# Lending tiles to one attention head, and issuing three small steps later, in a two-layer trunk kernel

## The chip, the cores and the metric

The kernel runs on one core of a Trainium2 chip. The metric is the device time of one execution in microseconds (us), the median of several runs. The profiled execution comes with a trace of every instruction; its times count from the first instruction of the core.

## The reference

Two layers of the same block work on 512 frames of width 1024, in float32:

```
xn = rmsnorm(x);  [u | q | k | v | gA | gB] = xn @ w_in
q, k = rotary(rmsnorm(q)), rotary(rmsnorm(k))           # 4 heads, each of two q/k pairs of width 128
p_c  = softmax(q_c k_c^T / sqrt(128), chunk-causal)     # c = 0, 1
o    = rmsnorm((p_0 - lam * p_1) v)                     # v of width 256 a head
pool = (windowed mean of u, minus u) @ w_pool           # windows 2, 4, 8, 16: one for each 256 columns
x    = x + (sigmoid(gA) * pool + sigmoid(gB) * o) @ w_out
x    = x + SwiGLU(rmsnorm(x))
```

## The kernel before

Every float32 product is made of three TensorE matmuls (`product`: high x high, high x low, low x high), for which both operands are split into a rounded high part and a remainder. ScalarE (ACT) makes the high part, VectorE (DVE) the remainder (`split`, L216). Weights are loaded as float32 pieces (`raw`, seven slots) and split into `whi` and `wlo` (six slots).

The work goes head by head in the order 3, 2, 1, 0 (`ORDER`). `attention(j)` projects q and k of a head for the four blocks t of 128 tokens, then v and a gate. `merged(j-before)` then does the pooling branch of the head before: two products for u, two for its gate, and two small ones with `pw` (called y here). A layer ends with the feed-forward part.

The steps of a head that follow the q/k projection of a block t are these, with the lines of the profile:

- `evicted`: squares of the accumulator on ACT (L623), a mean and a power -0.5 on DVE and POOL (L355, L356). Then `normed`: the scaling into `qn` on ACT (L628), and in the same step the rotation on DVE (`rotate`, L385 and L393), a 32x32 transpose into the tile `near` (L326), a store to DRAM (`away<-near`, L327) and four loads back (L331), which together transpose the block.
- `turn`: the transposed `near` is scaled (L533) and split into `qh`, `ql`.
- `scores`: two products into the two `sc` banks, a maximum (L548), and Exp into a probability tile `pr` (L549). `joined` subtracts the second softmax from the first (L553 to L555) and sends the result through the same store and loads. Its transposed copy lies in the second half of the same `pr` tile.
- `turn_prob`: that copy is split into `ah`, `al`. `weighted`: the product with v (`mm<-vh,ah` and so on), squares (L588), scaling (L592). `turn_out` (L611) writes the head's rows of `mj`.

The first head of layer 0 (`at_start`) transposes on TensorE instead. In layer 1 the first head's projections of t = 0 and t = 1 are both held until the statistics of the tokens are there, so the steps of these two blocks start at the same moment.

The order of the work comes from the program and from a planner that runs when the program is built. `clock` counts the matmul columns issued. `later(delay, step)` puts a step into a heap, and `run_due` issues the steps whose time has come, between two products. `need(keys)` issues steps from the heap, in order of their time, until all the keys are ready, even before their time. So a step issued later takes a later place in each in-order engine queue. All delays are in columns. The tile framework then hands out slots, places instructions and inserts the waits: a tile of a tag with n slots waits until the tile that had the slot is no longer read.

Slots that matter here: `qn` three (used by `qn` and by its `near`), `pr` two, `ah` and `al` one each, `ta` two, `us` and `up` two each, `m` two, `mt` three (used by `mt` and its `near`), `sc` two banks, `mm` six banks.

The pooling branch (`windowed`) scales u into `up` (L689), adds shifted copies in `us` (L694, up to four times), finishes the mean (L697 to L700) and splits it into `uh`, `ul` at once. The gate is scaled into `ta` on DVE (L718) and goes through Tanh on ACT (L719) at once.

Of the kernel before, what the change touches and what calls it, by code (L numbers as in the profile page):

```python
# [11 lines left out]
F32R = mybir.dt.float32r  # L12
BF16 = mybir.dt.bfloat16
AF = mybir.ActivationFunctionType
# [4 lines left out]
P = 128  # L19
D = 1024  # L20
S = 512
# [32 lines left out]
SCORE_WAIT, PROB_WAIT, AV_WAIT, NORM_WAIT, MERGE_WAIT = 33600, 25200, 11400, 15000, 15000  # L54

QK_AWAY, SCORE_AWAY, PROB_AWAY, AV_AWAY, MERGE_AWAY = 28000, 26000, 32000, 18000, 24000
NORMED, JOINED, GATED = 4800, 2400, 4800
HIDDEN_DELAYS = (26000, 28000), (8000, 14000)


# [64 lines left out]
def trunk_kernel(  # L125
# [138 lines left out]
    def later(delay, what):  # L264
        heapq.heappush(waiting, (clock[0] + delay, count[0], what))
        count[0] += 1
# [97 lines left out]
    def need(*keys):  # L364
        run_due(lambda: all(k in ready for k in keys))
# [12 lines left out]
    def rotate(qn, t, layer):  # L378

        cs, sn = rotary[layer]  # L380
        both = sb.tile([P, 4, 4, ROT], F32, name="m12", tag="m12")

        def by(to, x, table):
            to, x = (v.rearrange("p (a h) r -> p a h r", a=2) for v in (to, x))
            nc.vector.tensor_mul(to, x, table.unsqueeze(2).broadcast_to(list(x.shape)))  # L385

        m1, m2 = both[:, 0], both[:, 1]
        by(m1, qn[:, :, :ROT], cs[:, :, t, :])
        for a in range(2):
            b = (1 - a) * HALF  # L390
            here = slice(a * HALF, (a + 1) * HALF)
            by(m2[:, :, here], qn[:, :, b:b + HALF], sn[:, :, t, here])
        nc.vector.tensor_add(qn[:, :, :ROT], m1, m2)  # L393
# [105 lines left out]
    for layer in range(L):  # L499
# [14 lines left out]
        def attention(j, before, then):  # L514

            if before is not None:
                need(*((layer, before, "s", t) for t in range(NT)))
            norm_eps = {}
            qh, ql = pair("q", "qk", 4)
            mj = sb.tile([P, 2, S], F32, name="mj", tag="mj", bufs=2)  # L520
# [16 lines left out]
            def scores(t):  # L537
                width = (t + 1) * P
                pr = sb.tile([P, 2, S], F32, name="pr", tag="pr", bufs=2)
                prob = [pr[:, c, :width] for c in range(2)]  # L540
                st = small("st", 2)
                mx = small("mx", 2)
                for c in range(2):
                    sc = s_ps()
                    product(sc[:, :width], [(
                        (qh[:, c, token(t)], ql[:, c, token(t)]), (qh[:, 2 + c, :width], ql[:, 2 + c, :width]))])
                    nc.vector.memset(sc[:CHUNK, width - CHUNK:width], MASKED)
                    nc.vector.tensor_reduce(mx[:, c:c + 1], sc[:, :width], axis=AX.X, op=ALU.max, negate=True)  # L548
                    nc.scalar.activation(prob[c], sc[:, :width], AF.Exp, bias=mx[:, c:c + 1], accum_out=st[:, c:c + 1])  # L549
                norm_eps[j, t] = rc = small("rc", 2)  # L550

                def joined():
                    nc.vector.reciprocal(rc[:, 1:2], st[:, 1:2])  # L553
                    nc.vector.scalar_tensor_tensor(rc[:, 0:1], rc[:, 1:2], st[:, 0:1], neglam[layer], op0=ALU.mult, op1=ALU.mult)
                    nc.vector.scalar_tensor_tensor(prob[0], prob[1], rc[:, 0:1], prob[0], op0=ALU.mult, op1=ALU.add)  # L555
                    nc.scalar.activation(rc[:, 1:2], st[:, 0:1], AF.Square, scale=EPS ** 0.5 / (1.0 - lam_init))
                    if at_start:
                        later(PROB_WAIT + (4000 if t == NT - 1 else 0) - JOINED, lambda: turn_prob(t, prob[0]))
                    else:
                        near = turned(prob[0], t + 1, near=prob[1])  # L560
                        later(PROB_AWAY - JOINED, lambda: turn_prob(t, near))
                    ready.add((layer, j, "s", t))

                after(JOINED, joined)

            def turn_prob(t, pr):
                if at_start:
                    tp = tr_ps()
                    for k in range(t + 1):
                        transpose(tp[:, token(k)], pr[:, token(k)])  # L570
                apart = at_start and t % 2
                ah, al = (sb.tile([P, S], F32R, name="a" + p, tag="u" if apart else "a" + p, bufs=2 if apart else 1) for p in "hl")
                width = (t + 1) * P
                if at_start:
                    split(ah[:, :width], al[:, :width], tp[:, :width])
                else:
                    split(*(squares_of(x[:, :width].rearrange("p (k c) -> p k c", c=P)) for x in (ah, al)), pr)
                later(AV_WAIT if at_start else AV_AWAY, lambda: weighted(t, ah, al))
# [32 lines left out]
                    nc.scalar.activation(into[:, a], src[:, a], AF.Copy, scale=gain_column(layer, 2 + a))  # L611
                ready.add((layer, j, "mj", t))

            at_start = not layer and j == ORDER[0]
            if not at_start:
                w = wblock(KD)
            held = []
# [1 line left out]
            def evicted(t, acc):  # L619
                qn = sb.tile([P, 4, QK], F32, name="qn", tag="qn", bufs=3)  # L620
                ss = small("ss4", 4)
                for h in range(4):
                    nc.scalar.activation(qn[:, h, :], acc[:, h * QK:(h + 1) * QK], AF.Square, accum_out=ss[:, h:h + 1])  # L623
                r = rsqrt_mean(ss, QK, 4, (QK ** -0.5, 1.0), [stats[0][:, i, t:t + 1] for i in (3, 4)])

                def normed():
                    for h in range(4):
                        nc.scalar.activation(qn[:, h, :], acc[:, h * QK:(h + 1) * QK], AF.Copy, scale=r[:, h:h + 1])  # L628
                    rotate(qn, t, layer)
                    near = qn if at_start else turned(qn.rearrange("p h c -> p (h c)"), 4, "qn", 3)  # L630
                    later((17400 + 5700 * t if at_start else QK_AWAY) - NORMED, lambda: turn(t, near))

                after(NORMED, normed)

# [49 lines left out]
        def windowed(j, c, acc, uh, ul):  # L684

            window = WINDOWS[j]
            up = sb.tile([P, 16 + S], F32, name="up", tag="up", bufs=2)
            nc.vector.memset(up[:, :16], 0.0)
            nc.vector.tensor_mul(up[:, 16:], acc, rms_rows[layer])  # L689
            prev, step, n = up, 1, 0  # L690
            while step < window:
                cur = sb.tile([P, 16 + S], F32, name="us", tag="us", bufs=2)
                nc.vector.memset(cur[:, :16], 0.0)
                nc.vector.tensor_add(cur[:, 16:], prev[:, 16:], prev[:, 16 - step:16 + S - step])  # L694
                prev, step, n = cur, step * 2, n + 1
            head = sb.tile([P, 16], F32, name="head", tag="head", bufs=2)
            nc.vector.tensor_mul(head, prev[:, 16:32], inv_t[:, j, :])  # L697
            nc.vector.scalar_tensor_tensor(
                prev[:, 32:], prev[:, 32:], 1.0 / window, up[:, 32:], op0=ALU.mult, op1=ALU.subtract)
            nc.vector.tensor_sub(prev[:, 16:32], head, up[:, 16:32])  # L700
            split(uh[:, c, :], ul[:, c, :], prev[:, 16:])

        def merged(j, mj, mh, ml):

            w = wblock(KD)
            pw = pool_weights(j)
            uh, ul = pair("u", "u", 2)
            for c in range(2):
                acc = mm_ps()
                product(acc, list(zip(cut(w, c * P, (c + 1) * P), x_all())))  # L710
                windowed(j, c, acc, uh, ul)

            gates = []
            for c in range(2):
                acc = mm_ps()
                product(acc, list(zip(cut(w, VD + c * P, VD + (c + 1) * P), x_all())))
                ta = sb.tile([P, S], F32, name="ta", tag="ta", bufs=2)
                nc.vector.tensor_mul(ta, acc, rms_rows[layer])  # L718
                nc.scalar.activation(ta, ta, AF.Tanh, scale=0.5)  # L719
                gates.append(ta)  # L720
            need(*((layer, j, "mj", t) for t in range(NT)))
            for c in range(2):
                y = mm_ps()
                product(y, list(zip(cut(pw, c * P, (c + 1) * P), [(uh[:, a, :], ul[:, a, :]) for a in range(2)])))
                ta = gates[c]
                k = KD * layer + 2 * j + c
                nc.vector.scalar_tensor_tensor(ta, ta, 1.0, y, op0=ALU.add, op1=ALU.mult)
                nc.vector.scalar_tensor_tensor(ta, ta, scale[:, k:k + 1], mj[:, c, :], op0=ALU.mult, op1=ALU.add)
                split_half(mh[:, c, :], ml[:, c, :], ta)
# [340 lines left out]
```

## Time and profile before

| what | value |
|---|---|
| runs | 1389.18, 1390.28 and 1390.07 us; median 1390.07 us |
| profiled execution | 1389.85 us |
| its span, first to last instruction | 1388.1 us, so 1.75 us lie around it |
| TensorE (PE) busy | 1375.9 us, 99%, 6242 matmuls |
| VectorE (DVE) busy | 999.4 us, 72% |
| ScalarE (ACT) busy | 777.8 us, 56% |
| GpSimd (POOL) busy | 123.8 us, 9% |
| mean granted TensorE clock | 0.997 of full speed |

Busy time of an engine is the time in which it has an instruction in work. The page's other parts name what ended each idle time (the releaser). A row of the timeline gives start, duration, engine, line, operation, output<-inputs, shape and count; square brackets at its end give the idle time before it and the releaser. SPq is the sequence of DMA issues of SyncE.

### The profile page before, as it was taken

What the parts mean: (1) busy time and instruction counts of PE and PEld (TensorE: products, weight loads), DVE (VectorE), ACT (ScalarE), POOL (GpSimd) and SP (SyncE); (2) the same over time, 40 slices, a digit from 0 to 9 for tenths busy, and PEclk for the clock granted to TensorE, in tenths of its full rate; (3) what the DMA queues carried; (4) which work ended last, traced back from release to release, by engine and by line L of the source; (5) the groups of instructions that cost most, each with busy time, mean ns of one, the idle gap of its engine ahead of it and who ended that gap; (6) DMA issues with size and microseconds to landing.
All of it is one profiled execution on the core that took longest, in us unless ns stands there. A gap on an engine that the chain in (4) does not pass through costs nothing.

```text
span 1388.1 us, 18670 instructions
## 1 busy us (share of the span) xinstructions
PE 1375.9 (99%) x6242; PEld 1140.2 (82%) x6242; DVE 999.4 (72%) x1787; ACT 777.8 (56%) x1577; POOL 123.8 (9%) x155
## 2 busy tenths in 40 slices
PE   9999999999999999999999989999999999999999
PEld 7888888888888888888888778888888888888887
DVE  7668677677869768678657676776878687686782
ACT  7665554554766555554456645555557565555540
POOL 3010100000101001110010001000001011001100
PEclk9999999999999999999999999999999999999999
DMA  8344454444668868676333545545436688687731
GB/s 310 99 130 134 126 159 130 148 135 136 148 181 193 240 174 232 157 207 202 119 129 120 147 128 153 152 121 149 154 115 152 184 199 230 184 219 175 199 127 61
DMA packets 141072, 224.07 MB, mean 161 GB/s; under 512 B 41392, under 2 KB 88496, under 8 KB 140976
## 3 DMA queue, kind: packets, MB, share of 16 engines
q1 hardware_dynamic: 130464, 187.20, 42.4%
q0 software_dynamic: 9216, 33.56, 14.1%
q10 hardware_dynamic: 1296, 2.13, 0.6%
q8 instruction: 49, 0.80, 0.2%
q14 instruction: 47, 0.39, 0.1%
HBM read 193.59 MB, written 29.23 MB: 161 GB/s over the span
## 4 chain that ended last, share of the span: by engine, by line
PE 96%; DVE 2%; issue 1%; ACT 1%; DMA 0%; SPq 0%; POOL 0%; DVEq 0%; ACTq 0%; POOLq 0%
PE mm L293 14%; PE mm L294 14%; PE mm L292 14%; PE mm L313 14%; PE mm L312 14%; PE mm L311 14%; PE sc L292 3%; PE sc L294 3%; PE sc L293 3%; PE sc L311 1%; PE sc L313 1%; PE sc L312 1%; DMA res<-in_x_t 0%; PE mm L318 0%; DVE wlo L216 0%
## 5 line engine op out<-in xcount | busy, mean ns | idle before, releaser
L216 DVE TENSOR_TENSOR wlo<-raw,whi 128x1024 fp32r<-128x1024 f32 (+1 forms) x221 | 267.4, 1215 | 79.4 <-ACT whi L216 78.7
L216 ACT CAST whi<-raw 128x1024 fp32r<-128x1024 f32 (+1 forms) x221 | 231.0, 1051 | 145.3 <-PE mm L294 61.2
L311 PE MATMUL mm<-whi,xh 128*128 128x512 f32 x480 | 189.0, 394 | 0.0
L313 PE MATMUL mm<-whi,xl 128*128 128x512 f32 x480 | 187.3, 390 | 0.0
L312 PE MATMUL mm<-wlo,xh 128*128 128x512 f32 x480 | 187.1, 390 | 0.0
L293 PE MATMUL mm<-fl,whi 128*128 128x512 f32 (+1 forms) x356 | 137.6, 387 | 0.0
L294 PE MATMUL mm<-fh,wlo 128*128 128x512 f32 (+1 forms) x356 | 137.6, 387 | 0.0
L292 PE MATMUL mm<-fh,whi 128*128 128x512 f32 (+1 forms) x356 | 137.6, 387 | 0.0
L732 DVE TENSOR_TENSOR res<-mm,res 128x512 f32<-128x512 f32 (+1 forms) x145 | 98.2, 680 | 46.4 <-PE mm L294 41.6
L313 PEld LDWEIGHTS mm<-whi,xl 128*128 128x128 f32 x480 | 90.1, 188 | 19.0
L312 PEld LDWEIGHTS mm<-wlo,xh 128*128 128x128 f32 x480 | 90.3, 188 | 17.4
L311 PEld LDWEIGHTS mm<-whi,xh 128*128 128x128 f32 x480 | 90.2, 188 | 17.3
L242 POOL DMA_DIRECT2D wlo<-in_wts x64 | 56.2, 878 | 536.5 <-ACT wlo L241 352.3
L312 PE MATMUL mm<-xl,whi 128*128 128x512 f32 x256 | 100.4, 392 | 0.0
L311 PE MATMUL mm<-xh,whi 128*128 128x512 f32 x256 | 100.3, 392 | 0.0
L313 PE MATMUL mm<-xh,wlo 128*128 128x512 f32 x256 | 100.1, 391 | 0.0
L356 POOL TENSOR_TENSOR r<-r,mhalf 128x4 f32<-128x4 f32 (+1 forms) x64 | 51.9, 814 | 531.1 <-DVE r L355 524.2
L292 PE MATMUL mm<-whi,xh 128*128 128x512 f32 x224 | 87.1, 389 | 0.0
L293 PE MATMUL mm<-wlo,xh 128*128 128x512 f32 x224 | 87.1, 389 | 0.0
L294 PE MATMUL mm<-whi,xl 128*128 128x512 f32 x224 | 87.1, 389 | 0.0
L241 ACT ACTIVATE wlo<-raw 128x1024 fp32r<-128x1024 f32 x64 | 67.9, 1060 | 29.2 <-PE mm L293 26.2
L292 PEld LDWEIGHTS mm<-fh,whi 128*128 128x128 f32 x356 | 66.9, 188 | 13.7
(221 smaller groups left out, 2969.1 us busy)
## 6 DMA issues: line engine op xcount, KB each, us to landing
raw<-in_wts SPq DMA_DIRECT2D x243, 512.0 KB, 4.0
wlo<-in_wts POOLq DMA_DIRECT2D x64, 512.0 KB, 6.3
away<-near SPq DMA_DIRECT2D x72, 256.0 KB, 2.3
near<-away SPq DMA_DIRECT2D x288, 64.0 KB, 2.9
away<-near SPq DMA_DIRECT2D x28, 128.0 KB, 1.9
near<-away SPq DMA_DIRECT2D x112, 32.0 KB, 2.0
pwr<-in_pool_w ACTq DMA_DIRECT2D x8, 256.0 KB, 3.2
away<-pr SPq DMA_DIRECT2D x7, 256.0 KB, 2.0
```

The source lines that it names most:

```text
L216: return nc.scalar.copy(hi, src), nc.vector.tensor_sub(lo, src, hi.bitcast(F32))
L241: made[0] = nc.scalar.activation(lo, raw, AF.Copy, scale=-1.0)
L242: nc.gpsimd.dma_start(lo.rearrange("p a b -> p (a b)"), wts[piece_no], accum_op=ALU.add)
L292: nc.tensor.matmul(acc, lhsT=ah, rhs=bh, start=start, stop=False, **check)
L293: nc.tensor.matmul(acc, lhsT=ah, rhs=bl, start=False, stop=False, **check)
L294: last = nc.tensor.matmul(acc, lhsT=al, rhs=bh, start=False, stop=stop, **check)
L311: nc.tensor.matmul(acc, lhsT=ah, rhs=bh, start=i == 0, stop=False)
L312: nc.tensor.matmul(acc, lhsT=ah, rhs=bl, start=False, stop=False)
L313: last = nc.tensor.matmul(acc, lhsT=al, rhs=bh, start=False, stop=i == n - 1)
L356: nc.gpsimd.tensor_tensor(r, r, mhalf[:, :width], op=ALU.pow)
L732: return nc.vector.tensor_add(res[d][:, cs], acc, res[d][:, cs])
```

## The change

Four things are done. In layer 1's head 3 (`roomy`), the transposed probabilities go to a `ta` tile instead of the second half of `pr`; `ah` and `al` of t = 1 and t = 3 share an `m` tile; and the `near` of q and k of t = 1 and t = 3 is a `us` tile instead of a `qn` one. In all heads, the scaling of q and k is issued 7200 columns after the squares, not 4800 (`NORMED`), and the rotation with its transpose and DMAs becomes a step of its own, another 2400 columns later (`ROTATED`); `turn` keeps its place. In all pooling branches the split of the pool sums is issued 9600 columns later (`SUMMED`) and the Tanh of the gate 2400 columns later (`GATE`). The y products are issued after `need` has found the two splits and the two Tanhs issued, as well as `mj`.

```diff
-NORMED, JOINED, GATED = 4800, 2400, 4800
+NORMED, ROTATED, JOINED, GATED, SUMMED, GATE = 7200, 2400, 2400, 4800, 9600, 2400
...
+            at_start = not layer and j == ORDER[0]
+            roomy = layer and j == ORDER[0]
...
-                        near = turned(prob[0], t + 1, near=prob[1])
+                        near = turned(prob[0], t + 1, *(("ta", 2) if roomy else ()), near=None if roomy else prob[1])
...
-                apart = at_start and t % 2
-                ah, al = (sb.tile([P, S], F32R, name="a" + p, tag="u" if apart else "a" + p, bufs=2 if apart else 1) for p in "hl")
+                if at_start and t % 2:
+                    ah, al = (sb.tile([P, S], F32R, name="a" + p, tag="u", bufs=2) for p in "hl")
+                elif roomy and t % 2:
+                    both = sb.tile([P, 2, S], F32R, name="a", tag="m", bufs=2)
+                    ah, al = both[:, 0, :], both[:, 1, :]
+                else:
+                    ah, al = (sb.tile([P, S], F32R, name="a" + p, tag="a" + p) for p in "hl")
...
                 def normed():
                     for h in range(4):
                         nc.scalar.activation(qn[:, h, :], acc[:, h * QK:(h + 1) * QK], AF.Copy, scale=r[:, h:h + 1])
+                    after(ROTATED, rotated)
+
+                def rotated():
                     rotate(qn, t, layer)
-                    near = qn if at_start else turned(qn.rearrange("p h c -> p (h c)"), 4, "qn", 3)
-                    later((17400 + 5700 * t if at_start else QK_AWAY) - NORMED, lambda: turn(t, near))
+                    tag = ("us", 2) if roomy and t % 2 else ("qn", 3)
+                    near = qn if at_start else turned(qn.rearrange("p h c -> p (h c)"), 4, *tag)
+                    later((17400 + 5700 * t if at_start else QK_AWAY) - NORMED - ROTATED, lambda: turn(t, near))
...
-            split(uh[:, c, :], ul[:, c, :], prev[:, 16:])
+
+            def rounded():
+                split(uh[:, c, :], ul[:, c, :], prev[:, 16:])
+                ready.add((layer, j, "u", c))
+
+            after(SUMMED, rounded)
...
-                nc.scalar.activation(ta, ta, AF.Tanh, scale=0.5)
                 gates.append(ta)
-            need(*((layer, j, "mj", t) for t in range(NT)))
+
+                def bent(c=c, ta=ta):
+                    nc.scalar.activation(ta, ta, AF.Tanh, scale=0.5)
+                    ready.add((layer, j, "g", c))
+
+                after(GATE, bent)
+            need(*((layer, j, "mj", t) for t in range(NT)), *((layer, j, x, c) for x in "ug" for c in range(2)))
```

More of the change, by code (lines that the diff above doesn't have):

```diff
@@ L612, in turn_out @@
                 ready.add((layer, j, "mj", t))
-            at_start = not layer and j == ORDER[0]
             if not at_start:
```

## The prediction

> **What bounds the kernel.** I read the page's first part, then PE's waits, the busy time by stretches, the timeline of PE where it waits, and from there backwards the timelines of the engines it waits for.
>
> ```profile
> span 1388.1 us, 18670 instructions
> PE 1375.9 (99%) x6242; PEld 1140.2 (82%) x6242; DVE 999.4 (72%) x1787; ACT 777.8 (56%) x1577; POOL 123.8 (9%) x155
> ```
>
> PE is busy for all but 12.2 us, so a change that removes no matmul can gain only there. The waits of PE by line and releaser (total, times, longest), and two stretches of busy time (count in brackets, then granted clock, DMA share, GB/s):
>
> ```profile
> PE mm L313 <- DVE al L216: 4.3, 2, 3.9
> PE mm L311 <- ACT ah L216: 2.5, 1, 2.5
> 85.00:140.00 55.00, 55.00 (x265) 46.37 (x264) 45.62 (x104) 33.71 (x84) 3.02 (x4) 1.00 0.51 153
> 804.10:810.90 6.80, 5.88 (x14) 4.61 (x15) 6.14 (x23) 2.50 (x9) 0.78 (x1) 0.50 0.17 37
> ```
>
> 6.8 us of waits are for `ah` and `al`, the split probabilities. The stretch of layer 0 in which head 2 and the pooling of head 3 run (85 to 140) has no idle PE. The stretch 804.1 to 810.9 in layer 1 ran at half the clock. PE's timeline at the places:
>
> ```profile
> 765.46 0.39 PE L313 MATMUL mm<-whi,xl 128*128 128x512 f32 x1
> 768.34 0.39 PE L311 MATMUL mm<-vh,ah 128*128 128x256 f32 x1 [2.49 <-ACT ah L216]
> 769.85 0.39 PE L313 MATMUL mm<-whi,xl 128*128 128x512 f32 x1
> 770.60 0.39 PE L313 MATMUL mm<-vh,al 128*128 128x256 f32 x1 [0.36 <-DVE al L216]
> 800.71 0.39 PE L311 MATMUL mm<-xh,whi 128*128 128x512 f32 x1
> 805.02 0.58 PE L313 MATMUL mm<-vh,al 128*128 128x256 f32 x1 [3.92 <-DVE al L216]
> 810.98 0.39 PE L313 MATMUL mm<-xh,wlo 128*128 128x512 f32 x1
> 811.21 0.40 PE L311 MATMUL mm<-xh,whi 128*128 128x512 f32 x1
> ```
>
> At full clock a 512-column matmul starts every 0.23 us (810.98 to 811.21). The three places cost, start to start less 0.23: 2.65, 0.52 and 4.08 us, together 7.25. From 805.02 to 810.98 there are 5.96 us for the stretch's 14 matmuls, one of 256 columns: at full pace 13.5 x 0.23 = 3.1, so the half clock cost 2.9. **Everything to be won is 10.1 us, in layer 1's head 3 and the head behind it.**
>
> **Why it waits.** The first stall, head 3, t = 3 (DVE and ACT rows):
>
> ```profile
> 746.31 0.69 DVE L548 TENSOR_REDUCE mx<-sc 128x1 f32<-128x512 f32 x1
> 753.98 0.43 DVE L216 TENSOR_TENSOR al<-pr,ah 128x256 fp32r<-128x256 f32 x1
> 755.57 0.68 ACT L549 ACTIVATE pr<-sc,mx 128x512 f32<-128x512 f32 x1
> 758.84 0.70 DVE L326 STREAM_TRANSPOSE pr<-pr 128x512 f32<-128x512 f32 x1
> 767.65 0.64 ACT L216 CAST ah<-pr 128x512 fp32r<-128x512 f32 x1
> 719.69 0.68 DVE L216 TENSOR_TENSOR ql<-near,qh 128x512 fp32r<-128x512 f32 x1
> 720.41 0.71 DVE L326 STREAM_TRANSPOSE near<-qn 128x512 f32<-128x512 f32 x1
> ```
>
> The maximum was there at 747.0, but the Exp of t = 3 began at 755.57: both `pr` slots were taken, and that of t = 1 came free with its `al` at 754.41. So 8.6 us passed before it, and 12.1 from Exp to `ah`. Likewise the transposed q and k of t = 2 (720.41) started right after the `ql` of t = 0 had freed a `qn` slot (720.37). The second stall, head 2, t = 0, and the same two steps in layer 0 as the last two rows:
>
> ```profile
> 779.71 0.31 DVE L326 STREAM_TRANSPOSE pr<-pr 128x128 f32<-128x128 f32 x1
> 785.10 1.73 SPq L327 DMA_DIRECT2D away<-near  x3
> 786.92 0.40 SPq L327 DMA_DIRECT2D away<-pr  x1
> 793.10 1.86 SPq L331 DMA_DIRECT2D pr<-away  x4
> 800.68 0.69 DVE L689 TENSOR_TENSOR up<-mm,hg 128x512 f32<-128x512 f32 x1 [2.20 <-PE mm L313]
> 804.68 0.28 DVE L216 TENSOR_TENSOR al<-pr,ah 128x128 fp32r<-128x128 f32 x1
> 105.00 0.28 DVE L216 TENSOR_TENSOR al<-pr,ah 128x128 fp32r<-128x128 f32 x1
> 113.84 0.28 PE L311 MATMUL mm<-vh,ah 128*128 128x256 f32 x1
> ```
>
> The store was issued 6.9 us after its data was transposed, since SP issues in order and had three other stores ahead (785.10); the loads came another 6.2 us later. `al` then stood in DVE's queue behind the pool sums, which stood 2.2 us for PE. In layer 0 the same `al` was done 8.5 us before its product.
>
> **The change, part by part.** No instruction, byte or DMA is added or removed; slots and places in queues change. 512 columns are 0.23 us, so 2400 are 1.1, 4800 are 2.1 and 9600 are 4.3.
>
> *Lent tiles.* With `near` in `ta`, `pr` of t = 1 is free once it is transposed, not once it is split, so the Exp of t = 3 can follow its maximum at 747.0: 8.6 us earlier. The split of t = 1 no longer waits for the product of t = 0 to read `ah`, which the `m` tile unties. The Exp-to-`ah` time of 12.1 us then ends near 759, and PE wants the data at 765.7: room of 6 us against a stall of 2.65. The lenders are idle by what they do: `ta` is next written by the gates of the pooling, `m` by its result, `us` by its sums, and these start no sooner than the row at 800.68. Gain: 2.65 + 0.52 = 3.2.
>
> The second stall: the late stores ahead of `away<-pr` are those of head 3 and of q and k of head 2, which queued behind them. If head 3 runs 8 us earlier, layer 1's head 2 should stand as layer 0's, with 8.5 us in hand. Gain: 4.08 + 2.9 = 7.0. What would be late next is the `mt` ring, which is not widened (rivals).
>
> *Rotation later (32 blocks).* Three waits that it addresses, and the rows of one block, from the first square to the scaled q:
>
> ```profile
> L385 DVE TENSOR_TENSOR m<-qn,hg 128x128 f32<-128x128 f32 x32 | 9.3, 290 | 28.1 <-ACT qn L628 27.7
> 62.34 0.28 ACT L623 ACTIVATE qn<-mm 128x128 f32<-128x128 f32 x1 [0.76 <-PE mm L313]
> 66.51 0.27 DVE L385 TENSOR_TENSOR m<-qn,hg 128x128 f32<-128x128 f32 x1
> 75.92 0.51 ACT L533 ACTIVATE near<-near,scale 128x256 f32<-128x256 f32 x1 [0.49 <-DMA near<-away]
> ```
>
> DVE stood 28.1 us at 32 rotations, 0.9 each, for ACT. A rotation already started 4.2 us after the squares (62.34 to 66.51); the new place is 9600 columns = 4.3 us after them. So it moves by 0.1 us if DVE arrives in time, and by 2.1 if all of the delay counts. `turn` stands where it stood, and the trip from rotation to `turn` took 9.4 us (66.51 to 75.92) with ACT waiting 0.5. A later rotation moves the transpose, one store and four loads on SP's queue with it; behind `turn` on ACT's queue stand weight roundings. Cost between 0 and what the rival below says; I take 0, being nearer to the row.
>
> *Pool sums and Tanh later.* 16 of each. The last row pair is `ul` and its first reader in layer 1's first pooling:
>
> ```profile
> L216 ACT CAST uh<-us 128x512 fp32r<-128x512 f32 x16 | 10.0, 623 | 44.5 <-DVE us L700 31.5 <-DVE us L693 13.0
> 822.09 0.69 DVE L216 TENSOR_TENSOR ul<-us,uh 128x512 fp32r<-128x512 f32 x1
> 827.94 0.39 PE L312 MATMUL mm<-ul,pw 128*128 128x512 f32 x1
> ```
>
> ACT stood 44.5 us at 16 roundings, 2.8 each; placed 4.3 later, it finds them ready. Even if `ul` were 4.3 us later than its end at 822.78, it would beat its reader by 0.9. The slot of `us` is held longer, but 4.3 us is less than the 5.5 (24 matmuls) until the next sums. The Tanh is 1.1 later and read only behind the y product, so its cover is that product; if it is gone, at most 1.1 us for the last pooling of each layer. `need` may now issue steps up to 1.1 us ahead of their time; against 8.5 us of margin, nothing. Lower bound for this part: PE has no wait for these, so no gain by itself, except that `al` no longer stands behind them.
>
> **Sum.** 1389.85 - 3.2 - 7.0 = 1379.7 for the profiled execution; I add 0.3 for one short wait at a weight split (the 0.7 us margin of the last rival). The median is 0.22 above that execution: **1380.2 us**.
>
> One rule to weigh: the half clock came after an idle time of 3.92 us and not after one of 2.49. [...]
>
> **Rivals.**
>
> *The second stall stays, whole.* `al` may still be queued behind the pool sums, which the change does not reorder by itself. Only 3.2 us are gained: 1390.1 - 3.2 = 1386.9. For it speaks that DVE is an in-order queue in the rows above; against it, layer 0.
>
> *The second stall stays, but short.* By the rows the half clock comes between 2.49 and 3.92 us of idle time. A rest of 1 to 3 us keeps the clock: 1381 to 1383.5.
>
> *Nothing moves.* The `mt` ring takes over: `near` of the attention output holds a slot until `turn_out`, and late `mt` tiles delay the same DVE and SP queues. The stalls return at other rows: within 1387.3 to 1392.8.
>
> *Slower.* Rotation and its trip late by all of the 2.1 us: `turn`, first in ACT's in-order queue, then waits 0.5 + 2.0 for its loads, and the roundings of weights behind it come late. The tightest one in the trace, at layer 1's head 3 (two splits, and the matmul that reads the second):
>
> ```profile
> 716.27 2.36 DVE L216 TENSOR_TENSOR wlo<-raw,whi 128x1024 fp32r<-128x1024 f32 x2
> 719.33 0.39 PE L312 MATMUL mm<-wlo,xh 128*128 128x512 f32 x1
> ```
>
> The margin is 0.7 us (718.63 to 719.33). A standstill of 1.3 us there costs 0.6. Eight heads have three such changes of weights each; were all as tight, 24 x 0.6 = 14.4 us, and 1390.1 - 10.1 + 14.4 = 1394.4. It decides from 0.54 us at every change (24 x 0.54 = 12.9 = the gain and 2.8 more). Against it: rotations were already 4.2 us behind the squares. [...]
>
> **How the numbers follow.** Differences of 0.2%, 2.8 us, are about what a measurement here can tell from none: 1387.3 to 1392.8 is no change. Forecast (both stalls gone) 0.63; second stall short 0.08; whole 0.09; nothing moves 0.10; slower 0.10. That gives faster 0.79 (the whole-stall case ends close to the bound), same 0.11, slower 0.10. The range takes in the first three cases, 0.80: up to 1387.2, which is the whole-stall case with the 0.3 added. Down to 1378.0: all 10.1 without the 0.3, the 0.9 by which the fastest run (1389.18) lies under the median, and 1.1 for shorter waits of the same stage that PE's busy time hides. The likeliest case alone: 1378.5 to 1381.5.
>
> **What would show it.** Right: PE without waits for `ah` and `al`, clock 1.00 from 737 to 832, the Exp of head 3's t = 3 within 2 us of its maximum, `away<-pr` of head 2's t = 0 within 2 us of its transpose, L385's and `uh`'s waits for ACT and DVE gone, and a span near 1378. Wrong: PE waiting for `wlo`, `ql` or `ul`; a stretch at half clock; L533 waiting for its loads far longer.

## The result and the profile after

In one job on one chip the kernel before took 1389.62 us (median of four executions, the three known before and one more) and the changed kernel 1380.59 us (1380.28 to 1381.05): ratio 0.9937, 95% interval 0.9920 to 0.9954. The forecast was 1380.2. The profiled execution of the changed kernel took 1380.28 us, against 1389.85 before. Page of the changed kernel, span and first part:

```profile
span 1378.5 us, 18671 instructions
PE 1371.7 (100%) x6242; PEld 1138.8 (83%) x6242; DVE 995.6 (72%) x1787; ACT 774.9 (56%) x1577; POOL 129.2 (9%) x155
```

These are the same matmuls in a span 9.6 us shorter. PE's waits in the changed kernel (line and releaser, total us, times, longest):

```profile
PE sc L311 <- ACT pr L551: 1.6, 2, 1.0
PE mm L408 <- DVE us L703: 1.2, 1, 1.2
PE mm L440 <- DVE sq L436: 0.4, 1, 0.4
PE mm L311 <- ACT ah L216: 0.2, 1, 0.2
```

6.8 us of waits for `ah` and `al` have become 0.2. A wait for a score bank is new: 1.6 us. Busy time by stretches, before (first fence) and after (second):

```profile
737.00:800.00 63.00, 60.15 (x283) 49.52 (x282) 43.11 (x102) 42.03 (x128) 6.39 (x8) 1.00 0.50 154
800.00:832.00 32.00, 28.00 (x123) 22.77 (x122) 25.61 (x62) 12.52 (x29) 2.30 (x3) 0.89 0.38 115
```

```profile
737.00:800.00 63.00, 61.99 (x294) 51.70 (x293) 44.51 (x107) 42.66 (x132) 6.94 (x9) 1.00 0.47 139
800.00:832.00 32.00, 31.83 (x153) 26.52 (x152) 26.55 (x64) 14.70 (x39) 3.01 (x4) 1.00 0.55 173
```

11 and 30 more matmuls fit into the two stretches, and the granted clock of the second is 1.00, not 0.89. The two chains, in the changed kernel. First head 3, t = 3, on DVE, ACT and PE:

```profile
742.10 1.29 DVE L550 TENSOR_REDUCE mx<-sc 128x1 f32<-128x512 f32 x2
742.83 0.69 ACT L551 ACTIVATE pr<-sc,mx 128x512 f32<-128x512 f32 x1
756.47 0.65 ACT L216 CAST a<-near 128x512 fp32r<-128x512 f32 x1
762.95 0.28 PE L311 MATMUL mm<-vh,a 128*128 128x256 f32 x1
```

The Exp follows its maximum at once; before it waited 8.6 us. The split starts at 756.47, not 767.65, and PE does not wait for it. Then head 2, t = 0: transpose, store, the store of t = 1, loads, split, and the matmul that reads `al`:

```profile
780.85 0.32 DVE L326 STREAM_TRANSPOSE pr<-pr 128x128 f32<-128x128 f32 x1
782.41 0.36 SPq L327 DMA_DIRECT2D away<-pr  x1
785.43 0.32 SPq L327 DMA_DIRECT2D away<-pr  x1
788.19 4.04 SPq L331 DMA_DIRECT2D pr<-away  x8
795.52 0.30 ACT L216 CAST ah<-pr 128x128 fp32r<-128x128 f32 x1
796.26 0.28 DVE L216 TENSOR_TENSOR al<-pr,ah 128x128 fp32r<-128x128 f32 x1
796.66 0.33 PE L313 MATMUL mm<-vh,al 128*128 128x256 f32 x1
```

There is no stall, but hardly any room: `al` ends at 796.54 and is read at 796.66.

The starts of the n-th matmul in both traces show where the time was gained. The changed kernel is 0.7 us ahead before the first stall and 4.1 ahead after it. It loses 1.5 near 779, is 2.7 ahead before the second stall, and 9.6 after it and at the end.

### The profile page after: what moved, and what is told of

Same layout as the page of the kernel before. It is cut to its first block, busy times and chain, and to the rows that moved or that the text cites. A ratio compares the mean times of both kernels' runs of the same rounds, so it can differ in the third digit from the quotient of the medians.

```text
span 1378.5 us, 18671 instructions
## 1 busy us (share of the span) xinstructions
PE 1371.7 (100%) x6242; PEld 1138.8 (83%) x6242; DVE 995.6 (72%) x1787; ACT 774.9 (56%) x1577; POOL 129.2 (9%) x155
## 4 chain that ended last, share of the span: by engine, by line
PE 95%; ACT 1%; DVE 1%; issue 1%; DMA 0%; POOL 0%; SPq 0%; ACTq 0%; DVEq 0%; POOLq 0%
PE mm L293 15%; PE mm L294 14%; PE mm L292 14%; PE mm L311 14%; PE mm L313 14%; PE mm L312 14%; PE sc L292 3%; PE sc L294 3%; PE sc L293 3%; PE sc L311 1%; PE sc L312 1%; ACT whi L216 1%; PE sc L313 1%; DVE wlo L216 0%; PE mm L318 0%
## 5 line engine op out<-in xcount | busy, mean ns | idle before, releaser
L356 POOL TENSOR_TENSOR r<-r,mhalf 128x4 f32<-128x4 f32 (+1 forms) x64 | 57.4, 898 | 516.7 <-DVE r L355 503.0
```

The source lines that it names most:

```text
L356: nc.gpsimd.tensor_tensor(r, r, mhalf[:, :width], op=ALU.pow)
```

## The experiments

Each ratio is to the kernel before in the same job. The code cuts show only the lines that differ, in e8 from the kernel of e1, in all others from the changed kernel.

**The parts apart.** Theory A: the slots of layer 1's head 3 caused everything. B: the second stall hangs on the place of the pool sums. C: the parts only work together.

```diff
 # e1_tiles_only
+NORMED, ROTATED, JOINED, GATED, SUMMED, GATE = 4800, 0, 2400, 4800, 0, 0
 # e2_delays_only
+            roomy = False
 # e3_no_sum_delay
+NORMED, ROTATED, JOINED, GATED, SUMMED, GATE = 7200, 2400, 2400, 4800, 0, 2400
 # e4_no_rot_delay
+NORMED, ROTATED, JOINED, GATED, SUMMED, GATE = 4800, 0, 2400, 4800, 9600, 2400
```

> Only the lent tiles; scaling, rotation, pool sums and Tanh in their old places. Theory A (the slots of layer 1's head 3 caused both stalls): both stalls and the half clock go, 1380 to 1382 us, waits of PE for ah and al under 1 us. Theory B (the second stall hangs on the place of the pool sums ahead of al in DVE's queue, and the lent tiles only cure the first): 3.2 us gained, about 1386.5, and the wait for al near 795 to 805 us of the span is still 3 to 4 us, with a stretch at half clock. Theory C (the parts only work together): 1388 to 1391.

Measured: 1380.47 us, 0.9933 (0.9916 to 0.9949). The lent tiles alone give all of the gain. PE's wait for `al` in that kernel:

```profile
PE mm L313 <- DVE al L216: 1.1, 2, 0.9
```

> All four later places, no lent tile. Theory A: the ring of pr, ah and al in layer 1's head 3 is as before, both stalls stay, 1387 to 1391. Theory B: the first stall stays (2.5 to 3.2 us), the second and its half clock go: about 1383. Theory C: 1388 to 1391, as A.

Measured: 1387.68 us, 0.9987 (0.9978 to 0.9997), at the edge of A and not B's 1383. All stalls are still there, some shorter, and one for an `ah` at 817.38 is new:

```profile
PE mm L311 <- ACT ah L216: 3.1, 2, 2.1
PE mm L313 <- DVE al L216: 1.8, 2, 1.5
800.00:832.00 32.00, 29.41 (x140) 23.41 (x139) 28.04 (x67) 14.35 (x34) 2.70 (x4) 1.00 0.46 146
```

In place of the wait of 3.9 us for `al` there is one of 1.5, with the new one of 1.0, and in this execution no half clock followed. That is where the 2 us come from.

> The changed kernel with the pool sums split at once again. Theory A: within 1.5 us of the changed kernel, 1380 to 1382. Theory B: a wait for al of 3 to 4 us near 800 us of the span returns, with the half clock 1387, without it 1384.

Measured: 1381.46 us, 0.9941 (0.9926 to 0.9956), as A.

> The changed kernel with scaling and rotation at their old places (4800 columns, in one step). Theory A: within 1.5 us of the changed kernel, 1380 to 1382; DVE's wait at the rotation returns to some 28 us in total, off PE's path. Theory C (the parts only work together): 1383 or more, with a PE wait for ah, al or a score in layer 1's first two heads.

Measured: 1380.61 us, 0.9934 (0.9919 to 0.9949), as A. PE's waits are those of the lent tiles alone (1.1 us for `al`), not the 1.6 us for a score bank. B and C have fallen.

**One loan less.**

```diff
 # e5_no_ta
+                        near = turned(prob[0], t + 1, near=prob[1])
 # e6_no_m
+                elif False:
 # e7_no_us
+                    tag = ("qn", 3)
```

> The changed kernel without the ta loan: the transposed probabilities of layer 1's head 3 lie in pr again. Theory A1 (each link of the chain pr, near, ah holds t = 3 by itself, and the ta loan is the one that frees pr): the Exp of t = 3 waits for the al of t = 1 again, and starts 4 to 9 us after its maximum; the first stall returns in part, 1382 to 1387. Theory A2 (any one of the loans makes enough room): 1380 to 1381.5.

Measured: 1391.40 us, 1.0011 (1.0002 to 1.0021): worse than either theory said, a little above the kernel before. PE at t = 3 of head 3, and the two stretches at half clock (0.50 and 0.51, the number after POOL's count):

```profile
765.56 0.39 PE L311 MATMUL mm<-vh,a 128*128 128x256 f32 x1 [1.77 <-ACT a L216]
766.85 0.58 PE L313 MATMUL mm<-vh,a 128*128 128x256 f32 x1 [0.78 <-DVE a L216]
766.40:769.80 3.40, 2.95 (x12) 2.86 (x13) 3.37 (x8) 2.29 (x4) 0.00 (x0) 0.50 0.09 10
807.30:810.70 3.40, 3.40 (x10) 2.62 (x9) 2.84 (x11) 1.20 (x6) 0.00 (x0) 0.51 0.02 5
```

The step that A1 named is not where most of it is lost. The way of t = 3, from its Exp to its split:

```profile
747.86 0.69 ACT L551 ACTIVATE pr<-sc,mx 128x512 f32<-128x512 f32 x1
754.71 0.34 SPq L327 DMA_DIRECT2D away<-near  x1
755.57 1.88 SPq L331 DMA_DIRECT2D pr<-away  x4
761.16 0.28 ACT L629 ACTIVATE qn<-mm 128x128 f32<-128x128 f32 x1 [3.14 <-PE mm L313]
764.88 0.63 ACT L216 CAST a<-pr 128x512 fp32r<-128x512 f32 x1
```

The Exp starts 1.3 us after its maximum (746.57), not 4 to 9, as the split of t = 1 is early with the `m` loan. But its loads stand behind a store of q and k (754.71) on SP, and its split on ACT behind squares that wait 3.14 us for PE. So the split comes at 764.88, 8.4 us later than in the changed kernel. The rows show this order; no run isolates it.

> The changed kernel without the m loan: ah and al of t = 1 and t = 3 share the one slot with t = 0 and t = 2 again. Theory A1: the split of t = 1 waits for the product of t = 0 near 752 us of the span, the ta slot of t = 1 comes free only then, and t = 3 is late again: 1382 to 1387. Theory A2: 1380 to 1381.5.

Measured: 1383.85 us, 0.9957 (0.9942 to 0.9972), as A1. The first stall is back, 2.17 us long. The Exp of t = 3 is on time (743.88), but the split of t = 1 waits (753.42), and with it the transpose of t = 3 for its `ta` tile (754.33).

> The changed kernel without the us loan: near of q and k of t = 1 and t = 3 takes a qn slot again. Theory A1: q of t = 2 and t = 3 is 4 us later as before, but a score is wanted only 8 us or more after that; no stall, 1380 to 1381.5. Theory A3 (the loan of us is what frees SP's queue and the second head): the wait for al near 800 us returns, 1383 or more.

Measured: 1387.52 us (1385.43 to 1389.28), 0.9984 (0.9975 to 0.9994). My A1 expectation was wrong by 6 us. The SP and ACT queues show why; first the changed kernel's SP, then that of the kernel without `us` (count at the end of each row), then its ACT:

```profile
745.24 3.00 SPq L327 DMA_DIRECT2D away<-near  x2
748.45 3.69 SPq L331 DMA_DIRECT2D near<-away  x8
```

```profile
747.60 1.83 SPq L331 DMA_DIRECT2D near<-away  x4
749.52 4.82 SPq L327 DMA_DIRECT2D away<-near  x2
754.45 0.37 SPq L228 DMA_DIRECT2D raw<-in_wts  x1
754.86 4.04 SPq L331 DMA_DIRECT2D near<-away  x8
760.62 0.28 ACT L629 ACTIVATE qn<-mm 128x128 f32<-128x128 f32 x1 [3.65 <-DVE near L326]
761.63 0.63 ACT L216 CAST a<-near 128x512 fp32r<-128x512 f32 x1
```

With the loan, the probabilities of t = 2 and t = 3 come back in one run of eight loads from 748.45. Without it, the loads of t = 3 stand behind a second store, which the row 749.52 stretches to 754.34, and come from 754.86. Then the split stands on ACT behind squares that wait 3.65 us for a `qn` slot: it starts at 761.63, not 756.47. PE still gets it in time; its new waits, for a score's `qh` (1.9 us) and an `ah` (2.2 us), are in head 2. How the lateness reaches head 2 is read from these rows, not isolated.

> The ta and m loans alone, no us loan, all steps in their old places. Theory I (without the us loan q and k of t = 2 and t = 3 are 5 us late, and this alone upsets the order of SP's and ACT's queues): about 1387, as without us in the changed kernel, PE waits for qh or ah of 4 to 6 us. Theory J (the us loan is needed only together with the later rotation, which lengthens the time in which a qn slot is held): 1380 to 1382.

This drops `us` from the lent tiles alone (the edits of e1 and e7). Measured: 1385.77 us, 0.9974 (0.9963 to 0.9984). The loan is worth about 5 us without any later step (1380.47 with it, in another job), so J has fallen; but the waits are for `al` (2.0 us) and `ah` (1.8), not `qh`.

**What is late next.** One more loan, `up` for the transposed attention output.

```diff
 # e8_mt_loan (on e1), e9_after_mt_loan (on the changed kernel)
-                        near = turned(m, 2, "mt", 3)
+                        near = turned(m, 2, *(("up", 2) if roomy else ("mt", 3)))
```

> The lent tiles alone, with one more loan: in layer 1's head 3 the transposed attention output lies in an up tile instead of an mt one. Theory D (the mt ring is what is late next: it holds the queues of DVE and SP, and so causes the rest of PE's waits for al, 1.1 us, in head 2): the transposes of the attention output of t = 2 and t = 3 come 8 to 12 us earlier, PE's waits for al fall under 0.4 us, 1379 to 1380. Theory E (these waits are from DVE's load by pool sums alone): as with the lent tiles alone, 1380 to 1381.

Measured: 1378.97 us (1378.74 to 1379.22), 0.9922 (0.9907 to 0.9937): D by its time, and the fastest of all. PE has no idle time left in either stretch. Its busy time there, then the squares of t = 3 and the transpose of t = 2 with the lent tiles alone, and with the further loan:

```profile
737.00:800.00 63.00, 63.00 (x300) 52.62 (x300) 45.77 (x119) 43.17 (x135) 6.98 (x9) 1.00 0.45 135
800.00:832.00 32.00, 32.00 (x154) 26.90 (x153) 27.17 (x65) 15.15 (x40) 3.48 (x4) 1.00 0.52 166
```

```profile
773.31 0.38 ACT L595 ACTIVATE mt<-mm 128x256 f32<-128x256 f32 x1
777.67 0.44 DVE L326 STREAM_TRANSPOSE near<-mt 128x256 f32<-128x256 f32 x1
```

```profile
765.26 0.39 ACT L595 ACTIVATE mt<-mm 128x256 f32<-128x256 f32 x1
773.24 0.45 DVE L326 STREAM_TRANSPOSE near<-mt 128x256 f32<-128x256 f32 x1 [0.35 <-ACT mj L618]
```

The squares come 8.0 us earlier, the transpose only 4.4, less than I wrote: with two `up` slots it still waits for `mj` of t = 0. That of t = 3 comes only 0.8 earlier (778.63 to 777.80). So D holds for the waits, not for the size of its steps.

> The changed kernel, delays and all, with the loan of an up tile for the transposed attention output as well. Theory D (the mt ring is what was late next in the changed kernel): the wait for a score near 778 us (1.6 us with its neighbours) goes, 1379 to 1379.8. Theory H (this wait comes from the later rotation, which puts q of the second block of head 2 late whatever the ring): it stays, 1380 to 1381, and the delays cost about 1 us beside the tiles with the mt loan (1378.97).

Measured: 1379.78 us, 0.9930 (0.9913 to 0.9946). The wait near 778 us is gone, as D says. It is also gone without the later scaling and rotation (e4), so it takes both, and H is right in that part. One for a score bank in layer 0, 0.6 us, is left, which no kernel with the rotation at its old place has; the changed kernel has it too, in this row:

```profile
54.65 0.38 PE L311 MATMUL sc<-qh 128*128 128x256 f32 x1 [0.60 <-ACT pr L551]
```

**The later steps by themselves.**

```diff
 # e11_sums_late_only
+NORMED, ROTATED, JOINED, GATED, SUMMED, GATE = 4800, 0, 2400, 4800, 9600, 0     (roomy = False)
 # e12_rot_later
+NORMED, ROTATED, JOINED, GATED, SUMMED, GATE = 7200, 7200, 2400, 4800, 9600, 2400
```

> The kernel before with one thing changed: the pool sums split 9600 columns later. Theory F (this is what the delays alone gained, 2 us, since al then waits less behind the pool sums in DVE's queue and the half clock does not come): 1387 to 1388.5, no half clock. Theory G (the gain of the delays alone came from the rotation): 1389 to 1391, a wait for al near 800 us of about 4 us and the half clock after it.

Measured: 1388.98 us, 0.9997 (0.9988 to 1.0006): G, by its waits. The wait for `al` is 3.9 us long as before, and half clock follows:

```profile
PE mm L313 <- DVE al L216: 4.5, 3, 3.9
805.20:808.60 3.40, 3.08 (x8) 2.39 (x9) 2.48 (x12) 2.50 (x9) 0.78 (x1) 0.50 0.00 0
```

So the 2 us of the later steps without the loans do not come from the pool sums alone. They need the scaling and rotation or the Tanh, which were not tried apart.

> The changed kernel with the rotation another 4800 columns (2.1 us) later, 14400 after the squares; turn keeps its place. The slower rival of the prediction: turn stands for its loads in ACT's queue, weight roundings come late, 1386 to 1394 and waits of PE for wlo or whi. The forecast's view (the trip has room, the roundings are covered): 1380 to 1382, ACT's wait at L535 for its loads grows from under 10 us to some 30 us or more.

Measured: 1380.56 us, 0.9935 (0.9920 to 0.9950), as the changed kernel. ACT's idle time ahead of the scaling in `turn`, in the changed kernel, in this one, and with scaling and rotation at their old places (e4):

```profile
L535 ACT ACTIVATE near<-near,scale 128x256 f32<-128x256 f32 x28 | 14.2, 509 | 4.5 <-DMA near<-away 4.5
L535 ACT ACTIVATE near<-near,scale 128x256 f32<-128x256 f32 x28 | 14.3, 511 | 10.7 <-DMA near<-away 10.7
L535 ACT ACTIVATE near<-near,scale 128x256 f32<-128x256 f32 x28 | 14.2, 508 | 10.1 <-DMA near<-away 10.1
```

The 10.7 us over 28 blocks are 0.4 each, far from the 30 that I wrote, and PE does not wait for any `wlo` or `whi`. Nor does this wait measure how late the rotation is: it is as long with the rotation at its old place as with the latest one, and shorter between.

## Why the prediction was right, and where it was not

- **Place and size of the gain.** Right. The waits for `ah` and `al` and the half clock, 10.1 us by their rows, are gone but for 0.2 us, and the time fell by 9.0 (medians of one job; 9.9 was forecast) or 9.6 (profiled executions). By the starts of the matmuls, 3.4 us were gained at the first stall (3.2 forecast) and 6.9 at the second (7.0). That the sum came out within 0.4 us is in part luck: 1.5 us were lost near 779, where the forecast had 0.3 for another wait, and 0.7 gained ahead of the first stall, for which it had no term.
- **Which part carries it.** Right: the lent tiles alone give 1380.47. The later steps add nothing to them.
- **First stall.** Right as a step: the Exp no longer waits for a `pr` slot. Its way to the split took 13.6 us (742.83 to 756.47), not 12.1; the 6 us of room took that. But an early Exp is not enough: without `ta`, and without `m`, it comes at 747.86 and 743.88, and the stall stays. Wrong in its detail is the `us` loan. The prediction gave it no share and no reason for that. The transposed q of t = 2 gains 4 us by it (720.41 to 716.05), but without it 5 to 7 us are lost, and the rows point to the order of the SP and ACT queues.
- **Second stall, "layer 1's head 2 should stand as layer 0's, with 8.5 us in hand".** The stall went, but this term was mis-sized: 0.12 us in hand. The store follows its transpose by 1.2 us, not 6.9, as forecast. But its loads come another 5.8 later (788.19), about as before (6.2). SP has the store of t = 1 ahead of them, which comes at 785.43, as soon as its data is transposed (785.37), and then five other loads, each over 0.4 us to issue (3.69 for eight). The split starts at 795.52, straight behind other work in ACT's queue.
- **What is late next.** Right: the `mt` ring. Lending it a tile takes off what remained in layer 1 (e8), in the changed kernel all but 0.2 us (e9).
- **The 0.3 for a weight split.** Wrong place: PE waits for no split. It waits 1.6 us for score banks: 1.0 at 779.23, which takes the `mt` ring and the later scaling and rotation together (e9, e4), and 0.6 in layer 0, which comes with the later scaling and rotation.
- **Later steps at no cost and no gain.** Right in the sum, wrong in the mechanism. I wrote that ACT and DVE would find their data ready. The groups of the changed kernel show that they stand as long as before (44.5 and 28.1 us then):

```profile
L216 ACT CAST uh<-us 128x512 fp32r<-128x512 f32 x16 | 9.9, 621 | 51.5 <-DVE us L710 39.1 <-DVE us L703 12.4
L385 DVE TENSOR_TENSOR m<-qn,hg 128x128 f32<-128x128 f32 x32 | 9.3, 291 | 33.3 <-ACT qn L634 32.9
```

- **The slower rival.** It did not come even with the rotation 2.1 us later again (e12): PE waits for no rounding of weights. The forecast's sign for it, a longer wait at L533, is a poor one (e12).
- **The rival with a short second stall, "a rest of 1 to 3 us keeps the clock".** Wrong as a rule: half clock followed a wait of 1.92 us (e7) and one of 1.98 (e10); see the last section.

## What to carry to other kernels

When one engine is busy 99% of the span, list its few waits by place, add what the clock loses behind them (2.9 us in the kernel before), and that sum is about the whole prize (10.1 us by the rows here, 10.7 with the best kernel). A wait for data can be a wait for a slot far upstream: follow it back until an instruction starts right after another has freed its tile, then lend that chain a tile that lies idle at that time. Here the loan that the prediction gave no share, `us`, was worth 5 to 7 us (e10, e7): without it, loads stood on SP behind a store that took until 754.34, and a split on ACT behind squares that waited 3.65 us. So drop each loan once before calling it useless.

## What the runs showed of the hardware

In these runs half clock came behind waits as short as 1.92 us. PE's waits in layer 1's first two heads, the matmul that ended each (its start; the place of the one of 3.9 was not read), and the granted clock read there:

| kernel | wait of PE (us) | ended by the matmul at | granted clock |
|---|---|---|---|
| before | 2.49, then 0.36 | 768.34, 770.60 | 1.00 from 764 to 771 |
| before | 3.92 | 805.02 | 0.50 from 804.11 to 810.93 |
| sums late only | 3.9 | | 0.50 from 805.2 to 808.6 |
| without `ta` | 1.77, then 0.78 | 765.56, 766.85 | 0.50 from 766.4 to 769.8 |
| without `m` | 2.17 | 766.73 | 0.50 from 768.0 to 771.4 |
| without `us` | 1.92 | 781.25 | 0.50 from 783.3 to 786.7 |
| without `us` | 2.25 | 817.91 | 1.00 from 800 to 832 |
| `ta` and `m` only | 1.98 | 800.91 | 0.50 from 801.3 to 804.7 |
| delays only | 1.49; 1.03 | 803.28; 817.38 | 1.00 from 800 to 832 |

So a wait of 2.49 us kept the clock (the kernel before), and one of 1.98 cost it (`ta` and `m` only):

```profile
800.91 0.39 PE L313 MATMUL mm<-vh,al 128*128 128x256 f32 x1 [1.98 <-DVE al L216]
801.30:804.70 3.40, 3.40 (x9) 2.62 (x9) 2.07 (x9) 1.39 (x7) 0.00 (x0) 0.50 0.03 5
```

The length of the wait alone did not decide it in these runs, and none of them isolates what did. The stretches read at half clock are 3.4 us long, a loss of up to 1.7 each (an estimate: half of 3.4); in the kernel before it lasted 6.82.

The price was not the same in every execution of a kernel. Without `us`, two executions of ten took 1385.4 us at a mean clock of 1.000, and the longest 1389.28 at 0.997; with `ta` and `m` only, the shortest took 1384.06 at 1.000 and the longest, which is the profiled one, 1387.49 at 0.997. One stretch of 3.4 us at half clock is about 0.0012 of the mean clock, an estimate from 1.7 of some 1386 us. The 2.9 us that the prediction put on the half clock were thus the price in one execution of the kernel before.
